# The order of VectorE's operations in a quad of sums, and where the sums are put together

## The chip, the cores and the metric

The kernel runs on one core of one Trainium2 chip. The metric is the device time of one execution in microseconds (us). The time of the kernel before is the median of three runs.

## The reference

One layer of a decoder over 256 tokens with a width of 2048, all in fp32. Cut to what matters here:

```python
h = rms_norm(x, g_mix_pre)
aq, ak, av, hq, hf, hi, hg, gate_a, gate_b = split(h @ w_in)
y_attn = sliding_window_attention(rotary(aq), rotary(ak), av, sinks)
y_hgrn = rms_norm(hgrn2_recurrence(hq, hf, hi, lb), gnorm) * silu(hg)
merged = sigmoid(gate_a) * (y_attn @ w_attn_branch) + sigmoid(gate_b) * (y_hgrn @ w_hgrn_branch)
x = x + rms_norm(merged @ w_out, g_mix_post)
gate, up = split(rms_norm(x, g_ffn_pre) @ w_gate_up)          # 2048 -> 2 x 5632
x = x + rms_norm((silu(gate) * up) @ w_down, g_ffn_post)      # 5632 -> 2048
x = x + rms_norm((p @ w_ple_proj) * sigmoid(rms_norm(x, g_ple_pre) @ w_ple_gate), g_ple_post)
```

Nearly all the work is in the products with the weights.

## The kernel before

**Products.** The 256 tokens are two halves c of 128. Each fp32 product is made of three matmuls of rounded parts: with x = hi + lo and w = wh + wl they are wh·hi, wh·lo and wl·hi. One such matmul takes a chunk of 128 of the inner dimension k and 512 output columns (128x512 in the traces), and adds into one of TensorE's eight sum banks (PSUM, `acc`). Weights are streamed as `raw` tiles, a pair of two k chunks by 512 columns (512 KB), from SP's queue into a ring of six buffers. ACT makes wh as a copy of raw with rounding, VectorE makes wl = raw - wh. Activations are split in the same manner into hi and lo in tiles of 128x512 (four chunks of one half).

**Quads.** In 59 places two raw pairs form a quad: two k chunks by two blocks of 512 columns. b11 and b21 are the two chunks of the first block, b12 and b22 those of the second. In place of 8 products (2 halves x 2 chunks x 2 blocks, 24 matmuls) a quad has 7 (21 matmuls), with four sums of weight tiles, t1 = b11 - b12, t2 = b22 + t1, t4 = b21 - t2 and t3 = b22 - b12. VectorE makes the four sums, and each of the seven factors b11, b21, t1, t2, b22, t4, t3 gets its wh from ACT and its wl from VectorE (`wl<-raw,wh` or `wl<-t,wh`). That is `parts_of_quad`. On the other side of the product stand four sums of activation chunks, `sides`, with their parts shi and slo, made once per pair of chunks by `in_place_of_quad` (four VectorE operations of 128x128, a copy on ACT, one VectorE operation).

Quads appear in the last three pairs of blocks of w_in (the gates, "gate pairs"), in w_out, in gate and up (a block there is a gate and an up block of 512 columns) and in w_down. A block has quads and plain pairs mixed. The products of t1, t2, t3 and b11 add into four sum banks of their own over all quads of a block; the other products go to the four `cs` banks of the block itself (two column blocks by two halves).

**Putting the sums together.** After the last quad of a block (16 times) `put_together` copies the sum of b11 (p1, on ACT) and makes three tiles u2, u3, u4 with four VectorE operations that each read a sum bank and a u (`u<-acc,u`). `drop` gives a sum bank back. When the block is over, `total` adds each of the four cs banks to its u (again `u<-acc,u`) and drops the bank.

**What sets the order.** Each engine runs its instructions in program order, and the order is decided when the program is built. `clock` counts the time that TensorE's matmuls are reckoned to take. A helper written as a generator says with each `yield` when it wants to go on: after a number of us, or when the last operation of an engine, as reckoned, is over (`yield V` for VectorE, `yield A` for ACT, `yield T` for TensorE). The generators stand in a heap by due time, and `pump`, called after each group of matmuls, lets the due ones write their next instructions. `parts_of_quad` is advanced by `prefetch_quads` one `yield` at a time, while fewer than two sets of parts are ready or VectorE is reckoned to be done within 1.5 us; two quads may be under way, and then the older goes first. Slots, sum banks and raw buffers are given out in the order in which they come free. A group of transposes (`misc<-ident,u`) takes a bank only when at least three are free, so the moment at which a bank is dropped in the program also sets where such a group stands on TensorE.

`load_more` puts the next weight DMA on SP's queue; it starts when the raw buffer that it fills is released, which is when the last operation that reads it is over.

In the traces nearly every row has line 181, since one helper records all operations; rows are told apart by their tiles.

Of the kernel before, what the change touches and what calls it, by code (L numbers as in the profile page):

```python
# [17 lines left out]
ALU = mybir.AluOpType  # L18
# [110 lines left out]
def block_kernel(ctx: ExitStack, tc: tile.TileContext, I, out: bass.AP):  # L129
# [55 lines left out]
    V = InOrder(nc.vector, 0.07, 0.00105)  # L185
# [50 lines left out]
    def slot(s, shape=(P, NB), dt=F32):  # L236
        i = free_slots.popleft()
        t = slots.tile(list(shape), dt, tag=f"s{i}", name=nm(s))
        owner[id(t)] = i, t
        return t  # L240

    def free(*tiles):
        for t in tiles:
            free_slots.append(owner.pop(id(t))[0])

    def room(n):

        while len(free_slots) < n:
            yield 0.3
# [13 lines left out]
    def drop(ps):  # L263
        banks.append(bank_of.pop(id(ps))[0])
# [10 lines left out]
    def act(o, i, f, **kw):  # L275
        return A.activation(o, i, f, **kw)

    def tt(o, a, b, op):
        return V.tensor_tensor(o, a, b, op)
# [84 lines left out]
    def parts_of_quad():  # L364

        w, k, col, raw, _ = loaded.popleft()
        other = loaded.popleft()[3]
        b11, b21, b12, b22 = raw[:, 0, :], raw[:, 1, :], other[:, 0, :], other[:, 1, :]
        parts = {}

        def hi(name, src):
            parts[name] = slot("wh", dt=F32R)
            act(parts[name], src, AF.Copy)

        def total(a, b, op):
            t = slot("t")
            tt(t, a, b, op)
            return t

        def lo(name, src):  # L380
            h, t = parts[name], slot("wl", dt=F32R)
            tt(t, src, h.bitcast(F32), ALU.subtract)
            parts[name] = h, t

        hi("b11", b11)
        hi("b21", b21)
        yield
        t1 = total(b11, b12, ALU.subtract)
        hi("t1", t1)
        lo("b11", b11)  # L390
        yield
        t2 = total(b22, t1, ALU.add)
        hi("t2", t2)
        t4 = total(b21, t2, ALU.subtract)
        hi("t4", t4)
        yield
        lo("b21", b21)
        load_more()
        t3 = total(b22, b12, ALU.subtract)
        hi("b22", b22)  # L400
        yield
        hi("t3", t3)
        lo("t1", t1)
        lo("b22", b22)
        load_more()
        free(t1)
        yield
        lo("t2", t2)
        lo("t4", t4)
        free(t2, t4)  # L410
        yield
        lo("t3", t3)
        free(t3)
        ready.append(((w, k, col), parts, None))

    def load_more():
        if plan:
            load_pair()
# [3 lines left out]
    def begin():  # L422

        if not loaded or len(making) > 1:
            return
        if loaded[0][4]:
            if len(loaded) > 1 and len(free_slots) >= STEP + SPARE:
                making.append(parts_of_quad())
                next(making[-1])
        elif len(in_pool) <= SPLIT or len(free_slots) >= ROOMY:  # L430
            making.append(parts_of_pair())
            next(making[-1])
# [87 lines left out]
    def by_quads(w, n, order, lhs, sides, cs, sums, us, start=True, stop=True, evac=None):  # L520
# [4 lines left out]
        for i, (q, seven) in enumerate(order):  # L525
# [38 lines left out]
            if last:  # L564
                chain(put_together(sums, us))

    def put_together(sums, us):

        yield T
        yield from room(4)  # L570
        p1, u2, u3, u4 = (slot("u") for _ in range(4))
        act(p1, sums["b11"], AF.Copy)
        drop(sums["b11"])
        yield A
        tt(u2, sums["t2"], p1, ALU.add)
        drop(sums["t2"])
        tt(u4, sums["t1"], u2, ALU.add)
        yield V
        tt(u3, sums["t3"], u2, ALU.add)
        drop(sums["t3"])  # L580
        tt(u2, sums["t1"], u3, ALU.add)
        drop(sums["t1"])
        us.extend([[p1, u3], [u4, u2]])

    def total(us, n, c, ps):

        while not us:
            yield 0.3
        u = us[n][c]
        tt(u, ps, u, ALU.add)  # L590
        drop(ps)
        return u
# [1120 lines left out]
    for at, (pair, gi) in enumerate(DOWN):  # L1713
        if at % 5 == 0:
            ps, us = [[acc(), acc()] for n in range(2)], []
            sums = {"left": len(SEVEN_DOWN[pair])}
# [138 lines left out]
```

## Time and profile before

| what | value |
| --- | --- |
| median of three runs | 1489.03 us (1486.18 to 1490.61) |
| the profiled execution's own time | 1489.56 us |
| its span, from the first to the last instruction | 1487.5 us |
| mean granted clock of TensorE | 0.997 |
| TensorE (PE) busy | 1469.5 us, 99% of the span |
| VectorE (DVE) busy | 1239.9 us, 83% |
| ScalarE (ACT) busy | 888.9 us, 60% |
| GpSimd (POOL) busy | 62.9 us, 4% |
| moved by DMA | 314.59 MB, mean 211 GB/s |

Times are us from the start of the span. A row of a timeline has the start, the length, the engine, line and operation, output and inputs, the shape, and how many like operations stand together; in brackets the idle time before it and what ended that. The end of a matmul is modelled, and matmuls overlap.

### The profile page before, as it was taken

What the parts mean: (1) busy time and instruction counts of PE and PEld (TensorE: products, weight loads), DVE (VectorE), ACT (ScalarE), POOL (GpSimd) and SP (SyncE); (2) the same over time, 40 slices, a digit from 0 to 9 for tenths busy, and PEclk for the clock granted to TensorE, in tenths of its full rate; (3) what the DMA queues carried; (4) which work ended last, traced back from release to release, by engine and by line L of the source; (5) the groups of instructions that cost most, each with busy time, mean ns of one, the idle gap of its engine ahead of it and who ended that gap; (6) DMA issues with size and microseconds to landing.
All of it is one profiled execution on the core that took longest, in us unless ns stands there. A gap on an engine that the chain in (4) does not pass through costs nothing.

```text
span 1487.5 us, 19958 instructions
## 1 busy us (share of the span) xinstructions
PE 1469.5 (99%) x6838; PEld 1216.3 (82%) x6838; DVE 1239.9 (83%) x2043; ACT 888.9 (60%) x1417; POOL 62.9 (4%) x107
## 2 busy tenths in 40 slices
PE   9999999999999999999999999999999999999997
PEld 6888888888887888888888888888888887888885
DVE  6878958755999867977899999999988899997773
ACT  7755655566666645665655666565655666575661
POOL 2100000000000100000000000000000000010000
PEclk9999999999999999999999999999999999999998
DMA  9754544345576856866756676576677678797551
GB/s 342 257 188 155 171 141 128 114 128 170 184 240 227 309 185 201 272 227 199 252 182 219 205 238 213 174 230 206 215 239 268 214 252 270 214 336 260 192 188 56
DMA packets 159557, 314.59 MB, mean 211 GB/s; under 512 B 11072, under 2 KB 11520, under 8 KB 159456
## 3 DMA queue, kind: packets, MB, share of 16 engines
q1 hardware_dynamic: 153024, 293.38, 61.0%
q0 software_dynamic: 6256, 19.88, 3.7%
q8 instruction: 53, 0.87, 0.2%
q14 instruction: 48, 0.39, 0.1%
q10 hardware_dynamic: 176, 0.07, 0.0%
HBM read 298.08 MB, written 15.21 MB: 211 GB/s over the span
## 4 chain that ended last, share of the span: by engine, by line
PE 64%; DVE 4%; issue 2%; DMA 1%; ACT 1%; DVEq 0%; POOLq 0%; POOL 0%; ACTq 0%
PE acc L181 63%; DVE wl L181 2%; PE misc L181 1%; DVE u L181 1%; ACT wh L181 1%; DVE t L181 1%; DMA raw<-in_w_in 1%; DMA raw<-in_w_down 0%; DMA raw<-in_w_gate_up 0%; DVE eg L181 0%; DVE slo L181 0%; DVE lo L181 0%; ACT hi L181 0%; DVE sides L181 0%; DVE s L181 0%
## 5 line engine op out<-in xcount | busy, mean ns | idle before, releaser
L181 PE MATMUL acc<-wh,hi 128*128 128x512 f32 x1769 | 700.2, 396 | 3.6 <-DVE u L181 2.4
L181 DVE TENSOR_TENSOR wl<-raw,wh 128x1024 fp32r<-128x1024 f32 (+1 forms) x606 | 595.7, 1007 | 115.4 <-ACT wh L181 113.8
L181 PE MATMUL acc<-wl,hi 128*128 128x512 f32 x1769 | 690.0, 390 | 0.0
L181 PE MATMUL acc<-wh,lo 128*128 128x512 f32 x1769 | 688.9, 389 | 0.0
L181 ACT ACTIVATE wh<-raw 128x1024 fp32r<-128x1024 f32 (+1 forms) x606 | 514.3, 883 | 239.8 <-PE acc L181 101.6
L181 PEld LDWEIGHTS acc<-wl,hi 128*128 128x128 f32 x1769 | 332.0, 188 | 71.2 <-DVE wl L181 1.1
L181 PEld LDWEIGHTS acc<-wh,hi 128*128 128x128 f32 x1769 | 332.3, 188 | 70.6 <-DVE u L181 3.2
L181 PEld LDWEIGHTS acc<-wh,lo 128*128 128x128 f32 x1769 | 332.5, 188 | 66.6 <-issue 0.2
L181 ACT ACTIVATE wh<-t 128x512 fp32r<-128x512 f32 x236 | 145.6, 628 | 106.6 <-DVE t L181 85.9
L181 DVE TENSOR_TENSOR wl<-t,wh 128x512 fp32r<-128x512 f32 x236 | 152.2, 683 | 0.5 <-PE acc L181 0.5
L181 DVE TENSOR_TENSOR u<-acc,u 128x512 f32<-128x512 f32 x132 | 86.3, 684 | 18.8 <-PE acc L181 17.6
L181 PE MATMUL acc<-wh,shi 128*128 128x512 f32 x236 | 91.9, 390 | 1.2 <-ACT shi L181 1.2
L181 PE MATMUL acc<-wh,slo 128*128 128x512 f32 x236 | 91.9, 390 | 0.2 <-DVE slo L181 0.2
L181 PE MATMUL acc<-wl,shi 128*128 128x512 f32 x236 | 91.8, 389 | 0.0
L181 DVE TENSOR_TENSOR t<-raw,t 128x512 f32<-128x512 f32 x118 | 81.1, 687 | 3.7
L181 PEld LDWEIGHTS acc<-wh,shi 128*128 128x128 f32 x236 | 44.3, 188 | 10.8 <-ACT shi L181 1.6
L181 PEld LDWEIGHTS acc<-wh,slo 128*128 128x128 f32 x236 | 44.3, 188 | 9.7 <-DVE slo L181 0.5
L181 PEld LDWEIGHTS acc<-wl,shi 128*128 128x128 f32 x236 | 44.3, 188 | 9.2
L181 POOL DMA_DIRECT2D act<-actd x40 | 21.4, 538 | 601.9 <-DVE wl L181 402.4
L181 DVE TENSOR_TENSOR t<-raw,raw 128x512 f32<-128x512 f32 x59 | 40.3, 684 | 3.9 <-DMA raw<-in_w_gate_up 1.9
L181 DVE TENSOR_TENSOR t<-raw 128x512 f32<-128x512 f32 x59 | 40.3, 684 | 0.0
L181 DVE TENSOR_TENSOR lo<-act,hi 128x512 fp32r<-128x512 f32 x40 | 27.2, 684 | 8.1 <-ACT hi L181 8.0
(214 smaller groups left out, 852.1 us busy)
## 6 DMA issues: line engine op xcount, KB each, us to landing
raw<-in_w_gate_up SPq DMA_DIRECT2D x176, 512.0 KB, 4.6
raw<-in_w_in SPq DMA_DIRECT2D x152, 512.0 KB, 4.3
raw<-in_w_down SPq DMA_DIRECT2D x88, 512.0 KB, 5.5
raw<-in_w_out SPq DMA_DIRECT2D x32, 512.0 KB, 5.5
raw<-in_w_ple_gate SPq DMA_DIRECT2D x32, 512.0 KB, 5.1
act<-actd POOLq DMA_DIRECT2D x40, 256.0 KB, 5.6
raw<-in_w_attn_branch SPq DMA_DIRECT2D x16, 512.0 KB, 5.2
raw<-in_w_hgrn_branch SPq DMA_DIRECT2D x16, 512.0 KB, 5.1
```

The costliest lines, as they stand in the source:

```text
L181: return tc.keep_in_program_order(f(o, *a, **kw))
```

## The change

In a quad, VectorE's order was t1, wl of b11, t2, t4, wl of b21, t3, wl of t1, wl of b22, wl of t2, wl of t4, wl of t3. Now it is t1, t3, t2, wl of b11, wl of b21, t4, wl of t1, wl of t2, wl of b22, wl of t4, wl of t3, with one `yield` fewer. The first of the two raw pairs is released after the sixth operation (it was the fifth), the second after the ninth (it was the eighth). The order of ACT's copies stays but for their places relative to the yields.

In `put_together` the last sum was t1 + u3 with u3 = t3 + u2; now it is t3 + u4 with u4 = t1 + u2, which is the same. The bank of t1 is dropped earlier. In place of the one wait for VectorE there are two waits of 0.5 us.

```diff
@@ -387,30 +387,29 @@
         yield
         t1 = total(b11, b12, ALU.subtract)
         hi("t1", t1)
-        lo("b11", b11)
-        yield
+        t3 = total(b22, b12, ALU.subtract)
         t2 = total(b22, t1, ALU.add)
         hi("t2", t2)
+        yield
+        lo("b11", b11)
+        lo("b21", b21)
+        yield
         t4 = total(b21, t2, ALU.subtract)
         hi("t4", t4)
-        yield
-        lo("b21", b21)
         load_more()
-        t3 = total(b22, b12, ALU.subtract)
         hi("b22", b22)
+        lo("t1", t1)
+        free(t1)
         yield
         hi("t3", t3)
-        lo("t1", t1)
+        lo("t2", t2)
+        free(t2)
         lo("b22", b22)
         load_more()
-        free(t1)
         yield
-        lo("t2", t2)
         lo("t4", t4)
-        free(t2, t4)
-        yield
         lo("t3", t3)
-        free(t3)
+        free(t4, t3)
         ready.append(((w, k, col), parts, None))
 
     def load_more():
@@ -574,12 +573,13 @@
         yield A
         tt(u2, sums["t2"], p1, ALU.add)
         drop(sums["t2"])
+        yield 0.5
         tt(u4, sums["t1"], u2, ALU.add)
-        yield V
+        drop(sums["t1"])
         tt(u3, sums["t3"], u2, ALU.add)
+        yield 0.5
+        tt(u2, sums["t3"], u4, ALU.add)
         drop(sums["t3"])
-        tt(u2, sums["t1"], u3, ALU.add)
-        drop(sums["t1"])
         us.extend([[p1, u3], [u4, u2]])
 
     def total(us, n, c, ps):
```

Since due times and banks decide the order, other instructions move with these: of 1917 rows of VectorE's program (1919 after) 636 stand elsewhere, of ACT's 164, of SP's 18, of TensorE's 42, of GpSimd's none. Three places follow. The numbers behind the names count tiles and differ between the two programs.

Where the second gate pair gives way to the third, on VectorE before: wl of three sums and of a plain pair (128x1024), the four totals, and the wl of another plain pair.

```order
L181 TENSOR_TENSOR wl_4410<-t_4360,wh_4362 128x512
L181 TENSOR_TENSOR wl_4412<-t_4364,wh_4366 128x512
L181 TENSOR_TENSOR wl_4414<-t_4378,wh_4388 128x512
L181 TENSOR_TENSOR wl_4338<-raw_4304,wh_4337 128x1024
L181 TENSOR_TENSOR u_4350<-acc_3985,u_4350 128x512
L181 TENSOR_TENSOR u_4352<-acc_3984,u_4352 128x512
L181 TENSOR_TENSOR u_4351<-acc_3981,u_4351 128x512
L181 TENSOR_TENSOR u_4349<-acc_3980,u_4349 128x512
L181 TENSOR_TENSOR wl_4417<-raw_4322,wh_4416 128x1024
```

The same place after:

```order
L181 TENSOR_TENSOR wl_4412<-t_4377,wh_4379 128x512
L181 TENSOR_TENSOR wl_4414<-t_4347,wh_4390 128x512
L181 TENSOR_TENSOR u_4354<-acc_3987,u_4354 128x512
L181 TENSOR_TENSOR u_4356<-acc_3985,u_4356 128x512
L181 TENSOR_TENSOR u_4355<-acc_3984,u_4355 128x512
L181 TENSOR_TENSOR u_4353<-acc_3983,u_4353 128x512
L181 TENSOR_TENSOR wl_4335<-raw_4304,wh_4334 128x1024
L181 TENSOR_TENSOR wl_4417<-raw_4322,wh_4416 128x1024
```

The wl of the plain pair (`raw_4304`) has moved from ahead of the four totals to behind them; one of the wl<-t,wh stands earlier than the rows shown.

The end of a gate and up block with four quads, on VectorE before: the four operations of `put_together`, the wl of a plain pair, the four totals.

```order
L181 TENSOR_TENSOR u_7687<-acc_7371,u_7686 128x512
L181 TENSOR_TENSOR u_7689<-acc_7370,u_7687 128x512
L181 TENSOR_TENSOR u_7688<-acc_7372,u_7687 128x512
L181 TENSOR_TENSOR u_7687<-acc_7370,u_7688 128x512
L181 TENSOR_TENSOR wl_7710<-raw_7617,wh_7709 128x1024
L181 TENSOR_TENSOR u_7687<-acc_7338,u_7687 128x512
L181 TENSOR_TENSOR u_7689<-acc_7337,u_7689 128x512
L181 TENSOR_TENSOR u_7688<-acc_7334,u_7688 128x512
L181 TENSOR_TENSOR u_7686<-acc_7333,u_7686 128x512
```

The same place after:

```order
L181 TENSOR_TENSOR u_7685<-acc_7377,u_7684 128x512
L181 TENSOR_TENSOR u_7687<-acc_7376,u_7685 128x512
L181 TENSOR_TENSOR u_7686<-acc_7378,u_7685 128x512
L181 TENSOR_TENSOR u_7685<-acc_7378,u_7687 128x512
L181 TENSOR_TENSOR u_7685<-acc_7344,u_7685 128x512
L181 TENSOR_TENSOR u_7687<-acc_7342,u_7687 128x512
L181 TENSOR_TENSOR u_7686<-acc_7341,u_7686 128x512
L181 TENSOR_TENSOR u_7684<-acc_7340,u_7684 128x512
L181 TENSOR_TENSOR wl_7711<-raw_7621,wh_7710 128x1024
```

The wl of the plain pair has moved behind the totals, and the first total reads the u that the operation ahead of it writes. TensorE at the same place before, from the third matmul of the new block on (`acc` are the block's own sums, `misc` are transposes of parts of the block before):

```order
L181 MATMUL acc_7730<-wl_7581,hi_6377 128x512
L181 MATMUL acc_7730<-wh_7580,hi_6377 128x512
L181 MATMUL acc_7730<-wh_7580,lo_6378 128x512
L181 MATMUL acc_7730<-wl_7581,hi_6377 128x512
L181 MATMUL acc_7731<-wh_7580,hi_6507 128x512
L181 MATMUL acc_7731<-wh_7580,lo_6508 128x512
L181 MATMUL acc_7731<-wl_7581,hi_6507 128x512
L181 MATMUL acc_7731<-wh_7580,hi_6507 128x512
L181 MATMUL acc_7731<-wh_7580,lo_6508 128x512
L181 MATMUL acc_7731<-wl_7581,hi_6507 128x512
L181 MATMUL misc_7758<-ident,u_7290 128x128 x4
L181 MATMUL misc_7763<-ident,u_7292 128x128 x4
```

TensorE after, from the last matmul of the old block on:

```order
L181 MATMUL acc_7344<-wl_7567,hi_6633 128x512
L181 MATMUL misc_7735<-ident,u_7298 128x128 x4
L181 MATMUL acc_7745<-wh_7584,hi_6381 128x512
L181 MATMUL acc_7745<-wh_7584,lo_6382 128x512
L181 MATMUL acc_7745<-wl_7585,hi_6381 128x512
L181 MATMUL misc_7752<-ident,u_7300 128x128 x4
L181 MATMUL acc_7745<-wh_7584,hi_6381 128x512
L181 MATMUL acc_7745<-wh_7584,lo_6382 128x512
L181 MATMUL acc_7745<-wl_7585,hi_6381 128x512
```

The first group of transposes has moved from behind the twelfth matmul of the new block to ahead of its first, the second group to behind its third.

In the down projection, on VectorE before: t1, the four `sides` and `slo` of one pair of chunks, the quad's t2 and t4. The wl of t1 is the next row after these.

```order
L181 TENSOR_TENSOR t_11920<-raw_11818,raw_11864 128x512
L181 TENSOR_TENSOR wl_11924<-raw_11818,wh_11890 128x512
L181 SCALAR_TENSOR_TENSOR sides_11926<-act_11701 128x128
L181 SCALAR_TENSOR_TENSOR sides_11926<-sides_11926,act_11700 128x128
L181 TENSOR_TENSOR sides_11926<-act_11700,act_11701 128x128
L181 TENSOR_TENSOR sides_11926<-act_11700,sides_11926 128x128
L181 TENSOR_TENSOR t_11952<-raw_11864,t_11920 128x512
L181 TENSOR_TENSOR t_11956<-raw_11818,t_11952 128x512
L181 TENSOR_TENSOR lo_11938<-act_11848,hi_11937 128x512
L181 TENSOR_TENSOR slo_11928<-sides_11926,shi_11927 128x512
L181 TENSOR_TENSOR wl_11981<-raw_11818,wh_11892 128x512
L181 TENSOR_TENSOR t_11985<-raw_11864 128x512
```

The same place after, in two pieces that follow each other:

```order
L181 TENSOR_TENSOR t_11927<-raw_11828,raw_11872 128x512
L181 TENSOR_TENSOR t_11931<-raw_11872 128x512
L181 TENSOR_TENSOR t_11933<-raw_11872,t_11927 128x512
L181 TENSOR_TENSOR wl_11950<-raw_11828,wh_11898 128x512
L181 TENSOR_TENSOR wl_11952<-raw_11828,wh_11900 128x512
L181 TENSOR_TENSOR lo_11922<-act_11717,hi_11921 128x512
L181 SCALAR_TENSOR_TENSOR sides_11958<-act_11717 128x128
L181 SCALAR_TENSOR_TENSOR sides_11958<-sides_11958,act_11716 128x128
L181 TENSOR_TENSOR sides_11958<-act_11716,act_11717 128x128
L181 TENSOR_TENSOR sides_11958<-act_11716,sides_11958 128x128
L181 TENSOR_TENSOR lo_11942<-act_11849,hi_11941 128x512
L181 TENSOR_TENSOR lo_11976<-act_11850,hi_11975 128x512
```

```order
L181 SCALAR_TENSOR_TENSOR sides_11979<-act_11850 128x128
L181 SCALAR_TENSOR_TENSOR sides_11979<-sides_11979,act_11849 128x128
L181 TENSOR_TENSOR sides_11979<-act_11849,act_11850 128x128
L181 TENSOR_TENSOR sides_11979<-act_11849,sides_11979 128x128
L181 TENSOR_TENSOR slo_11960<-sides_11958,shi_11959 128x512
L181 TENSOR_TENSOR t_12003<-raw_11828,t_11933 128x512
L181 TENSOR_TENSOR wl_12011<-t_11927,wh_11929 128x512
```

The same `sides` (`act_11717` is what `act_11701` was) stand six operations behind t1 and no longer two, a second set of `sides` stands ahead of their `slo`, and the wl of t1 comes after t4, which now stands behind the `slo`.

## The prediction

> **What bounds the kernel now.** I read the table of engines first, then TensorE's waits, then the timelines of TensorE, VectorE (DVE) and ScalarE (ACT) at each place where TensorE stands still.
>
> ```profile
> PE 1469.5 (99%) x6838; PEld 1216.3 (82%) x6838; DVE 1239.9 (83%) x2043; ACT 888.9 (60%) x1417; POOL 62.9 (4%) x107
> ```
>
> The reader is to see that TensorE (PE) is busy for 99% of the span and VectorE for 83%: an operation of VectorE costs time only where TensorE waits for it. All the waits of TensorE that a result of the sums ends, with their total, their count and the longest:
>
> ```profile
> PE acc L181 <- DVE u L181: 2.4, 2, 1.6
> PE acc L181 <- ACT shi L181: 1.2, 1, 1.2
> PE misc L181 <- DVE u L181: 0.4, 1, 0.4
> PE acc L181 <- DVE slo L181: 0.2, 1, 0.2
> 466.52 0.39 PE L181 MATMUL acc<-wh,lo 128*128 128x512 f32 x1
> 466.75 0.39 PE L181 MATMUL acc<-wl,hi 128*128 128x512 f32 x1
> ```
>
> They are five stops, 4.2 us together. The last two rows (start, duration) are two neighbours in TensorE's timeline: each lasts 0.39 us by the modelled end, but the next starts after 0.23 us. Waits are counted from that end, so a stop behind a matmul really costs some 0.16 to 0.2 us more. I work with starts. Some 5.2 us, 0.35% of the span, is all that earlier results of VectorE can give back, even if all five stops go. About 0.3% of the time, 4.5 us, is what a measurement of this kernel can tell from no change.
>
> **The price of a direct forerunner.** VectorE's timeline, with the row of the group first (count, busy us and mean ns):
>
> ```profile
> L181 DVE TENSOR_TENSOR t<-raw,t 128x512 f32<-128x512 f32 x118 | 81.1, 687 | 3.7
> 866.59 1.41 DVE L181 TENSOR_TENSOR t<-raw,t 128x512 f32<-128x512 f32 x2
> 867.92 0.68 DVE L181 TENSOR_TENSOR wl<-raw,wh 128x512 fp32r<-128x512 f32 x1
> 419.06 2.73 DVE L181 TENSOR_TENSOR u<-acc,u 128x512 f32<-128x512 f32 x4
> 421.71 1.88 DVE L181 TENSOR_TENSOR wl<-t,wh 128x512 fp32r<-128x512 f32 x3
> 423.51 2.48 DVE L181 TENSOR_TENSOR u<-acc,u 128x512 f32<-128x512 f32 x4
> ```
>
> At 866.59 stand t2 and then t4, which reads t2; the next operation starts 1.33 us later. Three operations that read no forerunner take 1.80 us from 421.71 to 423.51, 0.60 each. So t4 was held back by 1.33 - 2 x 0.60 = 0.13, and began 0.73 after t2. Of the 118 operations in the first row half, 59, are such a t4, one per quad. In the 16 places where the sums are put together four u operations follow each other; at 419.06 they take 2.65 us until 421.71, two holds. The new order keeps the first (u4 still reads u2 next to it) and loses the second. That takes 59 x 0.13 + 16 x 0.13 = about 9.5 us off VectorE's own time, with the same number of operations. Beside TensorE's 99% this alone is worth nothing: VectorE idles for 17%, and that cover stays.
>
> The Trainium skill speaks against this term: VectorE: DVE Perf Modes, section "The DRAIN you can't avoid", says that an operation starts only when the pipe is empty behind the one before, that leaving out waits doesn't help, and that the count of operations is what to save. By it the hold would be in every operation alike and the 9.5 us would be zero. The trace doesn't agree: 0.60 us without and 0.73 with a direct forerunner.
>
> **Gate pairs: a gain.** TensorE stops twice as one pair of gate blocks gives way to the next. The pair's last four totals (u<-acc,u) free the PSUM banks that the next pair's first quad writes, and TensorE waits for the fourth. Its timeline, and VectorE's ahead of the second:
>
> ```profile
> 424.88 0.39 PE L181 MATMUL acc<-wl,hi 128*128 128x512 f32 x1
> 426.04 0.50 PE L181 MATMUL acc<-wh,hi 128*128 128x512 f32 x1 [0.78 <-DVE u L181]
> 465.06 1.22 DVE L181 TENSOR_TENSOR wl<-raw,wh 128x1024 fp32r<-128x1024 f32 x1
> 466.20 2.47 DVE L181 TENSOR_TENSOR u<-acc,u 128x512 f32<-128x512 f32 x4
> 468.73 0.50 PE L181 MATMUL acc<-wh,hi 128*128 128x512 f32 x1 [1.59 <-DVE u L181]
> ```
>
> The stops are 426.04 - 424.88 - 0.23 = 0.93 us and 468.73 - 466.75 - 0.23 = 1.75 us. At the first, the u operations at 419.06 come ahead of the totals at 423.51 without a gap, so one hold less there and one in a quad before it bring the fourth total forward by 0.26 us, and by more if earlier holds had left a backlog: I take -0.4, between 0 and -0.93. At the second, the 1024 wide wl at 465.06 (1.14 us until 466.20) stands ahead of the totals before and behind them now. With the two holds that is 1.4 us: I take -1.4, between -1.1 and -1.75. The moved wl belongs to a plain pair that TensorE reaches only after the next quad's 21 matmuls, 21 x 0.23 = 4.8 us on, so I cost its delay at nothing; without that cover it would be its 1.14 us.
>
> **Block boundaries of gate and up: a loss.** Four times (815, 899, 984 and 1068 us) a block with four quads ends. VectorE puts its sums together and makes the totals; the transposes of the block before (misc) wait for banks. The timeline, TensorE's and VectorE's rows by time:
>
> ```profile
> 810.10 2.73 DVE L181 TENSOR_TENSOR u<-acc,u 128x512 f32<-128x512 f32 x4
> 814.74 1.13 PE L181 MATMUL misc<-ident,u 128*128 128x128 f32 x8
> 886.29 0.69 DVE L181 TENSOR_TENSOR t<-raw,raw 128x512 f32<-128x512 f32 x1 [0.52 <-DMA raw<-in_w_gate_up]
> 891.48 0.69 DVE L181 TENSOR_TENSOR wl<-raw,wh 128x512 fp32r<-128x512 f32 x1 [0.70 <-ACT wh L181]
> 895.03 2.73 DVE L181 TENSOR_TENSOR u<-acc,u 128x512 f32<-128x512 f32 x4
> 897.68 1.21 DVE L181 TENSOR_TENSOR wl<-raw,wh 128x1024 fp32r<-128x1024 f32 x1
> 898.75 0.39 PE L181 MATMUL acc<-wl,hi 128*128 128x512 f32 x1
> 898.81 2.47 DVE L181 TENSOR_TENSOR u<-acc,u 128x512 f32<-128x512 f32 x4
> 899.55 1.25 PE L181 MATMUL misc<-ident,u 128*128 128x128 f32 x8 [0.42 <-DVE u L181]
> 1063.91 2.73 DVE L181 TENSOR_TENSOR u<-acc,u 128x512 f32<-128x512 f32 x4
> 1068.43 1.25 PE L181 MATMUL misc<-ident,u 128*128 128x128 f32 x8
> ```
>
> Before, both groups of transposes stand twelve matmuls (2.72 us) into the new block and need the banks of the first and the second total. At 899.55 the first total (898.81 + 0.69) came too late: 899.55 - 898.75 - 0.23 = 0.57 us, and the second cost some 0.15 more. The others came just in time, as at 814.74. I count 1.4 us for all four, the third and fourth by the second's pattern.
>
> Now the first group stands at the block's first matmul, in the bank of b11, which ACT has emptied long before. The second stands three matmuls later and still needs the second total. Time it from the first u (T0): 0.73 (hold), 0.60, 0.60, then the first total, which now reads its direct forerunner, 0.73 later, and the second total 0.60 on: it ends at T0 + 3.26 + 0.69 = T0 + 3.95, and TensorE starts about 0.05 after. TensorE is there 0.45 (first group) + 0.68 = 1.13 us after the block's start B. B is 814.74 - 2.72 = 812.02, then 899.55 - 0.57 - 2.72 = 896.26 and 1068.43 - 2.82 = 1065.6, so B - T0 is 1.92, 1.23 and 1.7 us. The stop is 4.00 - 1.13 - (B - T0): 0.95, 1.6 and 1.2 us; with the third like the last, 5.0 us. An earlier T0 takes from it. At 891.48 VectorE waits 0.70 us for ACT's copy; the new order takes out a hold in the quad and asks for that copy one operation later, so T0 comes up to 0.6 us sooner at three of the places and 0.2 at the first: 2.0 us. Against that, the raw buffers are now released after the sixth and the ninth operation of a quad, not the fifth and the eighth, so their DMAs (on SP's queue, same number) start some 0.5 us later; the wait at 886.29 says that a quad starts when its load lands. So the four stops cost between 3.0 and 5.0 us, against 1.4. I take +2.2 us, between +1.5 and +3.6. Behind the waiting transposes TensorE has the whole next block. In the other blocks a group of transposes moves about 32 us earlier, to a place where its source and its bank are ready; I cost that at nothing.
>
> **The down projection: a loss.** The stop at 1239.62 is for sides (shi, slo), made in a quad's stretch. VectorE's rows, ACT's, TensorE's:
>
> ```profile
> 1234.55 0.69 DVE L181 TENSOR_TENSOR t<-raw,raw 128x512 f32<-128x512 f32 x1 [0.32 <-DMA raw<-in_w_down]
> 1235.77 0.29 DVE L181 SCALAR_TENSOR_TENSOR sides<-act 128x128 f32<-128x128 f32 x1
> 1239.59 0.69 DVE L181 TENSOR_TENSOR slo<-sides,shi 128x512 fp32r<-128x512 f32 x1 [0.81 <-ACT shi L181]
> 1235.90 1.06 ACT L181 ACTIVATE wh<-raw 128x1024 fp32r<-128x1024 f32 x1 [5.04 <-DMA raw<-in_w_down]
> 1237.39 0.62 ACT L181 ACTIVATE hi<-act 128x512 fp32r<-128x512 f32 x1
> 1238.01 0.39 PE L181 MATMUL acc<-wl,hi 128*128 128x512 f32 x1
> 1239.62 0.50 PE L181 MATMUL acc<-wh,shi 128*128 128x512 f32 x1 [1.22 <-ACT shi L181]
> 1240.34 0.50 PE L181 MATMUL acc<-wh,slo 128*128 128x512 f32 x1 [0.22 <-DVE slo L181]
> 1240.68 0.39 PE L181 MATMUL acc<-wl,shi 128*128 128x512 f32 x1
> ```
>
> Before, t1 starts when its load lands (1234.55), and the four sides follow one operation later, 0.93 us in all. They were early; shi was late because ACT waited for a load until 1235.90. TensorE lost 1240.68 - 1238.01 - 3 x 0.23 = about 2.0 us by its third matmul. Now t3, t2, two wl and a lo (which needs ACT's hi, about 1237.5) stand ahead of the sides: 1234.55 + 5 x 0.60 = 1237.55 for the lo, sides from 1238.15 to 1239.1, shi on ACT until about 1240.1. Then two lo and a second set of sides stand ahead of slo: 1239.1 + 1.2 + 0.93 = 1241.2, done 1241.9. After slo come t4 and then the wl of t1, from 1242.4 to 1243.1, and TensorE wants that in its third matmul: 1243.15 instead of 1240.68, +2.5 us. It would be 0 if the quad met an earlier load, and +3 if that load came 0.5 us later; I take +2.5, since both gating rows are loads that the change doesn't move.
>
> **The sum.** -0.4 - 1.4 + 2.2 + 2.5 = +2.9 us; the other moves (one pair split in two 512 wide halves, transposes by a few matmuls) I take at 0, between -0.1 and +0.8. The profiled execution took 1489.56 us (span 1487.5 and 2.1 around it), 0.5 over the median of the three runs, 1489.03. So 1489.56 + 2.9 = 1492.5 on its own base and 1491.9 as a median.
>
> **The rivals.** (1) Only the gains: the sides come no later, because their load lands sooner, and the boundaries lose no more than before: -1.8, so 1487.2. For it speaks that the stops of 1.75 and 0.93 us are plain targets; against it, the order of the rows at the boundaries. (2) Slower: at each boundary the second group of transposes waits its full time, because the later release of the raw buffers eats the earlier T0: +3.5, and the down stage +3.0, gains -1.2: +5.3, so 1494.3. It decides from a load that lands 0.5 us later at the place of 886.29. (3) VectorE bounds the kernel after all, and its 9.5 us come off: 1479.5. The first table and the small sum of TensorE's stops speak against it. (4) No hold can be taken out: every operation of VectorE costs the same wherever its forerunner stands, and only places move. The gains are then -1.1 and -0.1, the boundaries and the down stage +2.5 each: +3.8, so 1492.8. The rows from 866.59 and 421.71 speak against it. This is what the rule in VectorE: DVE Perf Modes (the Trainium skill) would make of the change.
>
> **How the numbers follow.** Likeliest case 0.50, rival 1 0.20, rival 2 0.22, rival 3 0.04, rival 4 0.04. The predicted time is 1491.9, its own range 1490 to 1494. The range of all reaches from rival 1 to rival 2 with 1.5 us beyond each, since the three runs shown differ by 4.4 us: 1485.7 to 1495.8. Slower by over 0.3% (from 1493.5) takes 0.15 of rival 2's chance and 0.10 of the others': 0.25. Faster by as much (to 1484.6) takes rival 3 and 0.02 of rival 1: 0.06. Within: 0.69.
>
> **What would show it.** Pairs t2, t4 that no longer follow each other, and VectorE's busy time equal or shorter while TensorE's stays. TensorE's stops at about 425 and 467 us shrink to under 0.6 us each. Transposes that wait for a total near 813, 898, 983 and 1067 us, about 1 us each, say that the boundary step is right; none says it is wrong. A stop of over 4 us near 1240 us (shi, slo, wl) decides the down step. New stops elsewhere, or a time under 1487 us, make the prediction wrong.

## The result, and the profile after

The changed kernel took 1498.24 us (median of five runs, 1497.25 to 1504.21), against 1489.03 before (five runs, 1486.18 to 1490.61): a ratio of 1.0076, with a 95% interval of 1.0052 to 1.0099 (it weighs all runs; the ratio of the two medians is 1.0062). So it is slower by about 9 us by the medians, outside the predicted range of 1485.7 to 1495.8. The profiled execution, the shortest of the five, took 1497.25 us with a span of 1495.2, 7.7 us more than the span before. The accounts below are made on these two spans.

The table of engines of the changed kernel, and all waits of TensorE that a result of the sums or of the transposes ends (total us, count, longest):

```profile
PE 1471.9 (98%) x6838; PEld 1217.3 (81%) x6838; DVE 1238.5 (83%) x2045; ACT 883.4 (59%) x1419; POOL 62.9 (4%) x107
```

```profile
PE misc L181 <- DVE u L181: 5.7, 4, 2.0
PE acc L181 <- ACT actT L181: 3.0, 4, 0.7
PE acc L181 <- DVE u L181: 0.9, 2, 0.7
```

VectorE's busy time is about what it was (1238.5 against 1239.9 us), and TensorE is still the bound. The two stops of the gate pairs are left, and they are shorter (0.9 us by this count, 2.4 before). The stop in the down projection is gone. The one wait of transposes for a total (0.4 us) has become four (5.7 us), and new are four waits of matmuls for ACT's copy of a transposed tile (actT, 3.0 us), a kind that had no row before. TensorE's timeline at the third block end, VectorE's there, and TensorE's and ACT's ahead of the block's first quad at the first block end:

```profile
823.25 0.60 PE L181 MATMUL misc<-ident,u 128*128 128x128 f32 x4
824.59 0.50 PE L181 MATMUL acc<-wh,hi 128*128 128x512 f32 x1 [0.74 <-ACT actT L181]
...
983.68 0.60 PE L181 MATMUL misc<-ident,u 128*128 128x128 f32 x4
...
984.58 0.40 PE L181 MATMUL acc<-wl,hi 128*128 128x512 f32 x1
986.99 0.66 PE L181 MATMUL misc<-ident,u 128*128 128x128 f32 x4 [2.01 <-DVE u L181]
...
988.05 0.63 PE L181 MATMUL acc<-wl,hi 128*128 128x512 f32 x1
988.48 0.63 PE L181 MATMUL acc<-wh,hi 128*128 128x512 f32 x1
...
991.04 0.48 PE L181 MATMUL acc<-wh,hi 128*128 128x512 f32 x1
991.36 0.39 PE L181 MATMUL acc<-wh,lo 128*128 128x512 f32 x1
```

```profile
974.87 0.69 DVE L181 TENSOR_TENSOR t<-raw,raw 128x512 f32<-128x512 f32 x1 [0.88 <-DMA raw<-in_w_gate_up]
...
982.81 5.32 DVE L181 TENSOR_TENSOR u<-acc,u 128x512 f32<-128x512 f32 x8
```

```profile
823.94 0.60 ACT L181 ACTIVATE actT<-misc 128x512 f32<-128x512 f32 x1 [4.34 <-PE misc L181]
```

Three things are to be seen. First, the group of transposes at 986.99 stands three matmuls into the block and waits for the second total: 986.99 - 984.58 - 0.23 = 2.18 us. The other three places give 0.65, 1.77 and 1.76 in the same way, 6.4 us together. Second, at 823.25 four transposes stand right ahead of the quad, and the quad's first matmul starts only at 824.59, when ACT's copy (823.94 to 824.54) has emptied the bank that the transposes filled: it is the same bank. That is 0.99 us more than without a wait, at 824, 911, 1000 and 1087 us alike, 4.0 us together. Third, behind the stop of 2.18 us the matmuls follow each other at 0.43 us and no longer at 0.23 (988.05 to 988.48), for about 3 us, which costs 1.6 us.

The account of the two traces, by starts of matmuls:

| place | predicted | measured |
| --- | --- | --- |
| gate pairs (425 and 467 us) | -1.8 | -1.5 |
| second group of transposes at four block ends | +2.2 | +5.1 |
| first matmul of the next quad, same bank as a group of transposes, four times | 0 | +4.0 |
| slow stretch behind one long stop | 0 | +1.6 |
| down projection (1240 us) | +2.5 | -1.9 |
| sum | +2.9 | +7.3 |

The +5.1 is the 6.4 us of stops and 0.2 us within the second groups, less what the same four places lost before: 0.8 us ahead of the groups (0.57 of it at 899.55) and 0.7 us within them. The remaining 0.4 of the 7.7 us lies in gaps too small to assign.

### The profile page after: what moved, and what is told of

Same layout as the page of the kernel before. It is cut to its first block, busy times and chain, and to the rows that moved or that the text cites. A ratio compares the mean times of both kernels' runs of the same rounds, so it can differ in the third digit from the quotient of the medians.

```text
span 1495.2 us, 19927 instructions
## 1 busy us (share of the span) xinstructions
PE 1471.9 (98%) x6838; PEld 1217.3 (81%) x6838; DVE 1238.5 (83%) x2045; ACT 883.4 (59%) x1419; POOL 62.9 (4%) x107
## 4 chain that ended last, share of the span: by engine, by line
PE 60%; DVE 7%; issue 3%; ACT 1%; DMA 1%; DVEq 0%; POOLq 0%; POOL 0%; ACTq 0%
PE acc L181 59%; DVE wl L181 3%; DVE u L181 2%; DVE t L181 1%; PE misc L181 1%; DMA raw<-in_w_gate_up 1%; ACT wh L181 1%; ACT actT L181 0%; ACT u L181 0%; DVE eg L181 0%; DMA actd<-actT 0%; DVEq L181 0%; DVE s L181 0%; DVEq L1851 0%; DVE slo L181 0%
## 5 line engine op out<-in xcount | busy, mean ns | idle before, releaser
L181 ACT ACTIVATE actT<-misc 128x512 f32<-128x512 f32 x22 | 13.0, 596 | 53.8 <-PE misc L181 53.8
```

The costliest lines, as they stand in the source:

```text
L181: return tc.keep_in_program_order(f(o, *a, **kw))
```

## The experiments

Theory A: the loss is where the program puts transposes, and which bank they fill; VectorE's order only moves them. Theory B: it is the later release of the raw buffers, which the quad's new order brings. Theory C: one of the two halves of the change does it all.

**The quad's order alone** (`put_together` as before):

```diff
-        yield 0.5
         tt(u4, sums["t1"], u2, ALU.add)
-        drop(sums["t1"])
+        yield V
         tt(u3, sums["t3"], u2, ALU.add)
-        yield 0.5
-        tt(u2, sums["t3"], u4, ALU.add)
         drop(sums["t3"])
+        tt(u2, sums["t1"], u3, ALU.add)
+        drop(sums["t1"])
```

> Only the quad's order is new; put_together is as before. Program: at the ends of the four-quad blocks both groups of transposes stand behind the twelfth matmul, as before, but one group stands right ahead of the next quad's first matmul, which writes the bank that ACT has to empty first. Theory A (the loss is where transposes stand): no stop behind the block's third matmul (0 instead of 6.4 us in four places), four stops of about 1.0 us ahead of the quad; the down projection's stop of about 2 us comes back, since TensorE arrives there earlier than in the full change. Sum about +4, 1492 to 1496 us. Theory B (the loss is the later release of the raw buffers, which is in this half): nearly all of the +9 us is here, 1497 to 1499. Theory C (the sums' half does it all): 1488 to 1490.

Measured: 1494.94 us, ratio 1.0046 (1.0034 to 1.0059).

```profile
PE acc L181 <- ACT actT L181: 3.3, 4, 1.0
PE acc L181 <- DVE slo L181: 1.3, 1, 1.3
PE misc L181 <- DVE u L181: 1.1, 3, 0.5
```

As Theory A has it: the four waits for actT are there (1.0 to 1.3 us each by starts), the long stops at the block ends aren't (at most 0.65 us each), and a stop of 1.5 us is back in the down projection. Not in the account of Theory A: the gate pairs' stop at 425 us is longer than before (1.80 us against 0.93), while that at 467 us is under 0.3.

**The sums' half alone** (the quad's order as before; cut, the rest of the quad goes back in the same way):

```diff
         t1 = total(b11, b12, ALU.subtract)
         hi("t1", t1)
-        t3 = total(b22, b12, ALU.subtract)
-        t2 = total(b22, t1, ALU.add)
-        hi("t2", t2)
-        yield
         lo("b11", b11)
-        lo("b21", b21)
         yield
+        t2 = total(b22, t1, ALU.add)
+        hi("t2", t2)
         t4 = total(b21, t2, ALU.subtract)
         hi("t4", t4)
+        yield
+        lo("b21", b21)
         load_more()
+        t3 = total(b22, b12, ALU.subtract)
...
```

> Only put_together is new; the quad's order is as before. Program: the first and second group of transposes stand at the block's first matmul and behind its third, as in the full change, and both next groups right ahead of the next quad. Theory A: four stops of 1 to 2 us behind the third matmul (about 6 us together), four stops of about 1.1 us ahead of the quad, the stop at 467 us nearly gone (-1.4): +6 to +9, 1495 to 1498 us. Theory B (raw buffers): within 2 us of before, 1487 to 1491. Theory C: like the full change, 1497 to 1499, with stops in both kinds of places.

Measured: 1495.24 us, ratio 1.0049 (1.0036 to 1.0063).

```profile
PE acc L181 <- ACT actT L181: 3.5, 4, 1.1
PE misc L181 <- DVE u L181: 3.2, 4, 1.6
PE acc L181 <- ACT shi L181: 1.7, 1, 1.7
```

Both kinds of new stops are here, with no raw buffer released later. Theory B can't explain this half's +7 us, and Theory C falls by the two kernels together: each half alone puts transposes right ahead of a quad, so their losses don't add up.

**Another bank for the quad's first matmul**:

```diff
-            sums.update({k: acc() for k in ("t1", "t2", "t3", "b11")})
+            sums.update({k: acc() for k in ("b11", "t1", "t2", "t3")})
```

> The full change, but the quad's four sum banks are asked for in the order b11, t1, t2, t3 and not t1, t2, t3, b11: the bank that the transposes have just filled goes to t3, which TensorE writes 18 matmuls (4.1 us) later, and not to b11, which it writes next. The order of the instructions is the same. Theory A: the four stops of about 1.0 us at 824, 911, 1000 and 1087 us go, the stops behind the third matmul (6.4 us) stay: about 4 us below the full change, 1493 to 1495. Theory B and a theory in which these stops only take up slack of late loads: no change, 1497 to 1499, and the time waits elsewhere.

Measured: 1494.04 us, ratio 1.0042 (1.0029 to 1.0055), 4.2 us below the full change. The waits for actT are gone to the last one, and the transposes' waits for totals stay:

```profile
PE misc L181 <- DVE u L181: 5.8, 4, 2.0
```

The last bank asked for is the last to come free, and b11, asked for last, is written first. The same edit also took away the gate pairs' stop at 425 us, which I had not expected: there it was the same mistake, with the bank of the fourth total.

**The sums later in the program**:

```diff
-        yield 0.5
+        yield V
         tt(u4, sums["t1"], u2, ALU.add)
...
-        yield 0.5
+        yield V
         tt(u2, sums["t3"], u4, ALU.add)
```

> The full change, but put_together waits twice for VectorE (yield V) in place of twice 0.5 us. VectorE's order in the quad and in put_together is the new one; the sums come later in the program, so that both groups of transposes stand eighteen matmuls into the block and the next ones thirty-two us later, none ahead of a quad. Theory A: no stop at the block ends and none ahead of quads; the wl at the second gate pair stands ahead of the totals as before, so little is gained there; the down projection's stop is back or larger. 1487 to 1491 us. Theory B: raw buffers are released as late as in the full change, so 1496 to 1499.

Measured: 1490.49 us, ratio 1.0018 (1.0008 to 1.0027). VectorE's order in quads and sums is the full change's, and 7.7 of the 9.2 us are gone. What is left at the block ends is 0.7 to 1.0 us at three of them; no matmul waits for actT. The second row below is the gate pairs' stop at 425 us. The down projection has no stop, which I had expected to be back.

```profile
PE misc L181 <- DVE u L181: 1.9, 3, 0.8
PE acc L181 <- DVE u L181: 1.5, 1, 1.5
```

The profiled execution, 1488.61 us, is the shortest of the eleven. Where the others lose the 2 us that the ratio still shows, no trace tells.

**One wait for VectorE, ahead of the last sum**:

```diff
-        yield 0.5
         tt(u4, sums["t1"], u2, ALU.add)
...
-        yield 0.5
+        yield V
         tt(u2, sums["t3"], u4, ALU.add)
```

> The full change, but put_together keeps one wait for VectorE (yield V) ahead of its last sum in place of the two of 0.5 us. Program: the two groups of transposes stand six matmuls ahead of the new block and at its start, in banks that are emptied early, and one group right ahead of the next quad, in the bank that its first matmul writes. Theory A: no or short stops at the block ends, four of about 1.0 us ahead of the quads: 1490 to 1494 us. Theory B: 1496 or more.

Measured: 1491.41 us, ratio 1.0026 (1.0015 to 1.0037). No transposes wait at the block ends; three of the four stops ahead of quads are there, and by starts the gate pairs stop for 1.7 us at 425 us and the down projection for 2.2.

```profile
PE acc L181 <- ACT actT L181: 2.5, 3, 1.0
PE acc L181 <- DVE slo L181: 1.3, 1, 1.3
```

**The quad's order alone, with the other bank order** (the first and the third edit above together):

> The quad's new order alone, put_together as before, with the banks in the order b11, t1, t2, t3. Theory A: the four stops ahead of quads (about 5 us of the quad_only kernel's +6) go; what is left of the new order's own effect is the stop at the first gate pair (1.8 in place of 0.9 us), the second one (0.3 in place of 1.75) and the down projection (1.5 in place of 2): 1487 to 1491 us, within 0.3% of before. Theory B: still 1493 or more.

Measured: 1490.17 us, ratio 1.0015 (1.0006 to 1.0024). The waits for actT are gone. The stops at the gate pairs shrank to about 0.3 us each and that in the down projection went, against the expectation, and one of 1.5 us came at 1109 us. Here too the profiled execution (1488.55 us) is among the shortest of eleven, and what makes the median 2 us longer than before isn't shown.

**The full change without its two losses**: the bank order above, and in gate and up

```diff
-        pa = yield from transpose4(t)
+        pa = yield from misc()
+        yield 2.7
+        for i in range(4):
+            transpose(pa[:, cols(i)], t[:, cols(i)], ident)
```

> The full change with the banks asked for in the order b11, t1, t2, t3, and in gate and up the transposes of a tile stand 2.7 us of TensorE's reckoned time behind the place where they got their bank. VectorE's order is the full change's. At the four block ends the two groups now stand behind the twelfth and the fifteenth matmul of the new block. Theory A (the loss is where the transposes stand and which bank they fill): no stop at the block ends, none ahead of the quads, no slow stretch behind a stop; the gains of the gate pairs (about 2 us, with the stop at 425 us) and of the down projection (2 us) stay: 1483 to 1487 us, faster than the kernel before. Theory B (later loads): the stops come back elsewhere in gate and up, 1490 us or more.

Measured: 1486.18 us, ratio 0.9988 (0.9979 to 0.9997). No transposes wait any more and no matmul waits for actT. Against the expectation, the down projection's gain didn't stay: its two waits are back, 2.5 us by starts (0.91 and 1.60):

```profile
PE acc L181 <- DVE slo L181: 1.3, 1, 1.3
PE acc L181 <- ACT shi L181: 0.7, 1, 0.7
```

**The same two edits on the kernel before, and the bank order alone on it**:

> The kernel before with both edits of late_transposes (bank order, transposes 2.7 us later in gate and up) but VectorE's old order in the quad and in put_together. Theory A: only its four stops at the block ends go, about 1 us: 1487 to 1489 us, and late_transposes (1486.2 in the runs on record) is 1 to 3 us faster by its gate pairs. If VectorE's order brings nothing by itself, this kernel is as fast as late_transposes, 1485 to 1487.

Measured: 1484.02 us, ratio 0.9973 (0.9961 to 0.9984). This is below both expectations. It beats both kernels, and late_transposes too by the median.

```profile
PE acc L181 <- DVE u L181: 0.9, 1, 0.9
PE acc L181 <- DVE slo L181: 0.2, 1, 0.2
```

> The kernel before with the sum banks asked for in the order b11, t1, t2, t3. No group of transposes stands right ahead of a quad in that kernel, so Theory A says nothing changes: 1487 to 1490 us, ratio within 0.2% of 1. If the order of the banks does something by itself, 1486 or less.

Measured: 1485.94 us, ratio 0.9983 (0.9974 to 0.9992). My expectation missed: I had looked for transposes right ahead of quads alone. The bank order also takes the stop at 425 us (0.93 to 0), shortens the one at 467 (1.75 to 0.65) and the one in the down projection (1.9 to 0.45). So with the banks in good order and the transposes out of the way, VectorE's old order is if anything faster than the new one: 1484.02 against 1486.18, not measured side by side, and the intervals of the two ratios just overlap. The traces differ by about as much in the down projection alone (stops of 0.49 against 2.5 us); at the second gate pair it is the old order that stops, for 1.07 us. The order by itself brings no gain that these runs show.

**Why the last quad of a block starts late.** In the changed kernel its t1 stands nearer to the block's end than before (below). Two tries on top of late_transposes:

```diff
+        lo("b22", b22)
+        load_more()
         lo("t2", t2)
         free(t2)
-        lo("b22", b22)
-        load_more()
```

> The late_transposes kernel with one more edit in the quad: wl of b22 stands ahead of wl of t2, so that the second raw pair is released after the eighth VectorE operation of a quad, as in the kernel before, and not after the ninth. In the kernels with the quad's new order t1 of the last quad of a four-quad block starts 9.1 to 9.4 us ahead of the block's end (second to fourth block), in the two with the old order 10.0 to 10.7. Theory C (that is the later release of the second pair): back to 9.8 us or more here. Theory D (it is the release of the first pair or VectorE's own order): 9.0 to 9.4 as in late_transposes. Time in both cases 1485 to 1488 us, since no stop hangs on it in this kernel.

Measured: 1503.19 us, ratio 1.0100 (1.0086 to 1.0114), with t1 at 7.1, 6.0 and 5.7 us ahead of the block's end. Neither theory has that. (after_oneV, which has the new order, doesn't fit the range that I gave for it either; its leads stand below.) The edit moved much else in the program, and TensorE stops 2.9 us at 469 and 4.4 us at 1245 us:

```profile
PE acc L181 <- DVE u L181: 4.3, 4, 2.8
PE acc L181 <- ACT shi L181: 4.2, 1, 4.2
```

It tells nothing on the question.

```diff
-NS = 61
+NS = 59
-SPLIT, LOADED, PACE = 6, 6, 2.3
+SPLIT, LOADED, PACE = 6, 7, 2.3
```

> The late_transposes kernel with seven raw buffers in place of six (and two working tiles fewer). VectorE's order in quads and sums, and the places of the transposes at the block ends, are the same. Theory C2 (in gate and up the last quad starts late against TensorE because a load waits for a raw buffer that the new order releases later): t1 of that quad starts 9.8 us or more ahead of the end of the second to fourth block, where late_transposes has 9.1 to 9.2, and the down projection's stop (2.5 us in late_transposes) shrinks: 1483 to 1486 us. Theory D (the lead is set by VectorE's and ACT's own work, or the load's own time): still 9.0 to 9.4 us, and 1485 to 1488.

Measured: 1483.84 us, ratio 0.9972 (0.9961 to 0.9983). No stop over 0.3 us is left in gate and up or in the down projection, which fits a load that waited for a buffer there (the two working tiles fewer can have had a part). So the new order with a seventh buffer is as fast as the old order with six in before_late (ratios of 0.9972 and 0.9973); the old order with seven was not run. Of the three leads one is 10.2 us, two are 9.15 as in late_transposes, though none of these t1 rows waits for a load here: at those two places the short lead isn't a load's doing in this kernel. What sets it stays open.

**Stops put in on purpose**, on the kernel before (nine of ten found a place; the chain of VectorE copies between two small matmuls is extra work; the diff is cut to that chain):

```diff
+        T.matmul(ps[:, :64], stop_t[:, :P], stop_t[:, :64], start=True, stop=True)
+        V.tensor_copy(stop_t[:, :64], ps[:, :64])
+        for _ in range(n):
+            V.tensor_copy(stop_t[:, 64:], stop_t[:, :64])
+        T.matmul(ps[:, :64], stop_t[:, :P], stop_t[:, :64], start=True, stop=True)
```

> The kernel before with ten stops of TensorE put in on purpose: at ten places a small matmul waits for a chain of 0 to 24 small VectorE copies (128x64) that starts from a matmul's result. In the full change matmuls ran at 0.43 us in place of 0.23 for some 3 us behind a stop of 2.2 us, at a granted clock of 0.50, but not behind stops of 1.8 us. If the length of the stop decides, all stops over 2.0 to 2.1 us have the slow stretch behind them and cost 1.6 us more, and none of the shorter ones; if it was chance, long stops without it or short ones with it are seen.

Measured, one run of 1563.98 us: of the stops put in, the one of 1.5 us has no slow stretch behind it, that of 2.28 has one (1.6 us), that of 2.42 has none, and all six from 3.3 to 7.6 us have one. So the length alone doesn't decide near the edge. What does is seen when the trace is cut where the clock changes. In this trace the half clock begins at 611.17, 669.19, 699.91 and 754.53 us, to name four, and lasts 3.41 us or twice that; the distances are 17, 9 and 16 times 3.413 us. In steps of 3.41 us from 607.75 and from 638.47 (length, TensorE's busy time, granted clock, DMA share, GB/s):

```profile
607.75:611.17 3.42, 1.42 (x8) 1.00 0.86 309
611.17:614.58 3.41, 3.41 (x10) 0.50 0.06 25
638.47:641.89 3.42, 2.94 (x15) 1.00 1.02 377
641.89:645.30 3.41, 1.74 (x9) 1.00 0.80 308
645.30:648.71 3.41, 3.41 (x17) 1.00 0.00 1
```

The stop of 2.28 us lies within one step and leaves TensorE 1.42 us of busy time in it; the next step has half the clock. The border of two steps at 641.89 cuts the stop of 2.42 us in two, neither step is below 1.74 us, and the clock stays.

## Why the prediction was wrong, by its own steps

**The direct forerunner: right, and worth nothing.** In the changed kernel t1, t3, t2 and the first wl follow each other at 0.60 us (989.18, 989.78, 990.38, 990.98 in VectorE's timeline):

```profile
989.18 0.69 DVE L181 TENSOR_TENSOR t<-raw,raw 128x512 f32<-128x512 f32 x1
989.78 0.68 DVE L181 TENSOR_TENSOR t<-raw 128x512 f32<-128x512 f32 x1
990.38 0.69 DVE L181 TENSOR_TENSOR t<-raw,t 128x512 f32<-128x512 f32 x1
990.98 1.29 DVE L181 TENSOR_TENSOR wl<-raw,wh 128x512 fp32r<-128x512 f32 x2
```

t2 still reads t1, but not next to it, and no hold is left among the four. (The 75 holds of 0.13 us would make 9.75 us, not 9.5; VectorE's busy time, in which overlapping operations count once, fell by 1.4 us, so the sum can't be read from it.) From t1 to the first u it takes 7.93, 7.93, 7.93 and 8.08 us at the four block ends, against 8.06, 8.74, 8.46 and 8.60 before: 2.0 us less together, which is just what I took off. The Trainium skill (VectorE: DVE Perf Modes, section "The DRAIN you can't avoid") says that an operation doesn't start until the pipe is empty; I read that too strictly, since the same section says that a next operation that isn't held starts earlier. The trace agrees with the latter: the rows above last 0.68 or 0.69 us and start 0.60 us apart.

**Gate pairs: right in sum, by the second stop.** The stops went from 0.93 and 1.75 us to 0.84 and 0.36:

```profile
425.10 0.39 PE L181 MATMUL acc<-wl,hi 128*128 128x512 f32 x1
426.17 0.50 PE L181 MATMUL acc<-wh,hi 128*128 128x512 f32 x1 [0.68 <-DVE u L181]
...
466.87 0.39 PE L181 MATMUL acc<-wl,hi 128*128 128x512 f32 x1
467.46 0.50 PE L181 MATMUL acc<-wh,hi 128*128 128x512 f32 x1 [0.20 <-DVE u L181]
```

The second fell by 1.4 us as forecast, because the wl now stands behind the totals; the first hardly moved (-0.1, not -0.4) and stays above the 0.6 us that I had named as a sign. What it hung on is the order of the banks: b11's is the one of the fourth total, and after_b11first has no stop there.

**Block ends: the mechanism right, the term mis-sized.** The step that failed is "an earlier T0 takes from it", the credit of 2.0 us. The quad did get shorter by 2.0 us, but its t1 started later against the block's end, so less than nothing was left. Its row at 974.87 names the load as what it waited for (0.88 us; the same row before, at 971.10, waited 0.39). t1 stood 9.98, 9.96, 10.05 and 10.37 us ahead of it before, and 10.34, 9.21, 8.80 and 9.38 after, 2.6 us worse together. At the third block end that is 983.68 - 974.87 = 8.8. I had written that a later release of the buffers works against the earlier T0, and set it at 0.5 us each; it is about 1 us from the second place on. Whether those releases do it is open. The quad's order has to do with it: t1 stands 9.1 to 9.3 us ahead at the second to fourth place with the new order alone, and 10.4 to 10.7 with the old one and the new sums. But the order doesn't bring it by itself. after_oneV has the new order too, and there t1 stands 10.9 to 12.1 us ahead, of which the group of transposes that comes six matmuls ahead of the block explains less than 0.5. A smaller part: from the first u to the start of the transposes it took 986.99 - 982.81 = 4.18 us at all four ends, not 4.00. The full formula with these numbers, 4.18 - 1.13 - 0.87 = 2.18 us, is the stop at the third end to the hundredth. For all four the full wait without any credit was 5.0 us by the forecast; 0.6 us for the later T0 (2.6 - 2.0) and 0.7 us for the 0.18 us four times make the 6.4 us measured.

**"A group of transposes moves about 32 us earlier, to a place where its source and its bank are ready; I cost that at nothing": wrong.** Source and bank were ready, and the transposes didn't wait. I left out who waits behind them: the next matmul takes the same bank, since a group that has just got one of four free banks leaves three for a quad that asks for four. The price is the transposes' and the copy's own time, 0.44 + 0.60 us, less a little: 0.99 us, four times. The kernel with the other bank order shows it by itself.

**The down projection: the chain right as far as slo, its anchor and its last link wrong.** Sides come 3.6 us behind t1 and slo 3.1 behind the sides, as computed (3.6 and 3.05). But I held t1's load fixed ("the change doesn't move" it). Against TensorE it came 3.6 us earlier than before, and slo was there just in time:

```profile
1240.63 0.69 DVE L181 TENSOR_TENSOR t<-raw,raw 128x512 f32<-128x512 f32 x1 [0.46 <-issue]
...
1244.25 0.28 DVE L181 SCALAR_TENSOR_TENSOR sides<-act 128x128 f32<-128x128 f32 x1
...
1247.33 0.69 DVE L181 TENSOR_TENSOR slo<-sides,shi 128x512 fp32r<-128x512 f32 x1
1247.93 0.68 DVE L181 TENSOR_TENSOR t<-raw,t 128x512 f32<-128x512 f32 x1
1248.53 1.29 DVE L181 TENSOR_TENSOR wl<-t,wh 128x512 fp32r<-128x512 f32 x2
```

```profile
1247.96 0.39 PE L181 MATMUL acc<-wh,shi 128*128 128x512 f32 x1
1248.19 0.40 PE L181 MATMUL acc<-wh,slo 128*128 128x512 f32 x1
1248.43 0.39 PE L181 MATMUL acc<-wl,shi 128*128 128x512 f32 x1
```

slo ends at 1248.02, and its matmul stands at 1248.19 with no wait ahead of it. Nor does TensorE want the wl of this t1 in its third matmul: that one starts at 1248.43, ahead of the wl at 1248.53. In the program the sides and the slo belong to the products of the quad before, whose wl stands further up. So the chain ends at slo, and the forecast's own times would make +1.6 us (slo done at 1241.9 instead of 1240.3), not +2.5. In quad_only t1 came 0.8 us later against TensorE, and 1.5 us of stop were back; in late_transposes 1.3 us later, and 2.5 us. So stops for sides and slo are real in kernels in which t1 is not early. Here it was early. TensorE's own delay of 9.6 us by then is not the reason, since after_VV, with 1 us of delay, has the same lead and no stop either. Why the load came early stays open.

**The slow stretch** was in no step.

**Luck.** The sum was off by 4.8 us on the two spans, and its terms by more: +2.9 at the block ends, +4.0 for the bank, +1.6 for the slow stretch, +0.3 at the gate pairs and 0.4 unassigned, against -4.4 in the down projection. That term was wrong in mechanism, and by luck it hid nearly half of the rest.

Rival 2, slower by +5.3, named the right place (block ends, full wait) and was still 4 us short, since it had neither the bank nor the slow stretch; its +3.0 in the down projection didn't come.

## What to carry to other kernels

When a change moves work on an in-order engine, ask of each moved instruction not only what it waits for but who takes its buffer next: here a group of transposes that waited for nothing cost 1 us each time, because the next matmul wrote the same bank. Ask for buffers in the order in which they are used; the first asked for should be the first written. A stretch of work that gets shorter helps only if its start stays where it was, so price its start and its length apart.

## What the runs showed of the hardware

A stop of TensorE of little more than 2 us can cost more than itself. In the changed kernel the granted clock was 1.00 through the stop, then 0.50 for one step of 3.41 us, and 1.00 again:

```profile
984.40:987.81 3.41, 1.40 (x9) 1.00 0.20 77
987.81:991.23 3.42, 3.42 (x10) 0.50 0.57 161
991.23:994.64 3.41, 3.41 (x17) 1.00 0.63 228
```

(The columns are the length, TensorE's busy time, the granted clock, the DMA share and GB/s.) The stops of 2.12, 2.12 and 2.18 us in two kernels and of 2.92 and 4.36 in a third all had such a stretch behind them, 1.6 to 1.7 us of loss each behind the first three; of single stops up to 1.87 us none had.

In all fourteen traces the clock changes only on a grid of 3.413 us, and TensorE's busy time in one step of the grid tells the clock of the next, between the start-up and the end of the program: at most 1.62 us in each of the 17 steps that have half a clock behind them, at least 1.64 us in all others. (A step is 3.41 us, and the busy time is the profile's, with its modelled ends.) So a stop counts by the idle time that falls into one step, and near the edge it matters where the borders fall: 2.18 us in one step had a slow stretch behind them, 2.42 us across a border had none. The borders lie differently in each execution: the clock first rises at 4.77 us of the span in the changed kernel's trace and at 4.54 in that of before. The two longest of the five runs of the changed kernel, 1501.76 and 1504.21 us, have the lowest mean clocks, 0.996 and 0.995 against 0.997 and 0.998; that fits more such steps in them, but no trace of theirs shows it.

The Trainium skill (TensorE: Matmul & The Clock Gate, section "Part 1: The HAM clock gate (the "warmup" mystery)") has the half clock after at least one idle window of about 3.4 us, and a window that runs freely. The trace agrees with the length of the window and with its running freely. It doesn't agree that the window has to be idle: 1.4 us of busy time in it were not enough to keep the clock.
